# Two neighbouring steps of a Strassen-type double exchanged in the second feed-forward stage

## The chip, the core and the metric

The kernel runs on one core of a Trainium2 chip. The metric is the device time of one execution in microseconds (us). Its engines are named as in the profile: PE is TensorE, the matrix engine (PEld its weight loads), DVE is VectorE, ACT is ScalarE, POOL is GpSimd, and SP is SyncE, which here only issues DMA transfers. Each engine works through its own instructions in order, and they wait for one another through semaphores. Matmuls add into banks of PSUM, 128 partitions by 512 fp32 values each. ACT and DVE read the banks.

## What is computed

One encoder layer on 512 tokens of width 1024: a half-weighted gated feed-forward stage, a mixer (dilated window attention, grouped-query attention, gates), a second feed-forward stage, and a final normalisation. Only the second feed-forward stage matters here:

```python
def rmsnorm(x, g):
    xf = x.astype(jnp.float32)
    y = xf * lax.rsqrt(jnp.mean(xf * xf, axis=-1, keepdims=True) + EPS)
    return (y * g.astype(jnp.float32)).astype(x.dtype)

def swiglu(x, w1, w3, w2):
    return (jax.nn.silu(x @ w1) * (x @ w3)) @ w2
...
        x = x + hybrid_mixer(h, w_in[l], b_gate[l], q_norm[l], k_norm[l], rel_bias,
                             w_branch_a[l], w_branch_b[l], w_out[l], cos, sin)
        x = x + 0.5 * swiglu(rmsnorm(x, ffn2_norm[l]), ffn2_w1[l], ffn2_w3[l], ffn2_w2[l])
    return rmsnorm(x, final_norm)
```

x is 512 by 1024, w1 and w3 are 1024 by 2816, w2 is 2816 by 1024, all fp32.

## The kernel before

**Products.** Activations are kept with features on partitions and tokens along the free axis. Each fp32 operand is split into a high part and the rest (names end in H and L). A product is three matmuls: high by high (L258), high weights by low activations (L259), low weights by high activations (L260).

**Doubles.** The 2816 hidden features are 22 chunks of 128. The kernel takes two neighbouring chunks f and f + 1 of w1 and w3 as a 2 by 2 block product, the inner dimension and the tokens being halved too, and computes it in the Strassen-Winograd way, with seven block products in place of eight. This is called a double. Its seven steps are named A11, S1, S2, A12, S3, S4, A22; each is 24 matmuls of 128 by 256. A double uses three banks: A, which A11 opens and which S2, S3 and A22 add to; Y, which S1 opens and S4 adds to; X for A12. Bank A comes from a pool of four (in the profile: mm), X and Y from another pool of four (X, Y), out of which also come the bank of the statistic (stat) and that of its transposes (rb).

**Evictions.** After every step the bank's sum so far goes out (`evict`): ACT copies it after A11 (L510), S1 (L512) and S2 (L514), DVE adds it to such a copy after A12 (L516), S3 (L521) and S4 (L530), and multiplies after A22 (L538). After S4, L533 multiplies by R, the row norms, and L534 applies silu.

**Order.** PE runs in the order in which the program is written; `slots` makes it. Double number i of a group has its step j at slot 7i + 2j, so that two doubles interleave. In the first group of the second stage, `ahead` is true, and a list of numbers puts the first steps in another order. S1(2) below is step S1 of the double whose first chunk is 2.

**Weights.** The same list orders the weights, since each step needs its own 128 by 1024 tile. A11 and A12 are loaded as they are (raw tile wa); the tiles of S1 and S3 are the sum of two loads (wt: SP issues the first, and POOL one that adds onto it, L225); those of S2 and S4 are added on DVE (ws, L242: S2 from S1's and A11's raw tile, S4 from S2's and A12's); A22 is loaded (wr). Then ACT casts the raw tile to the high part (wh, L243) and DVE subtracts to get the rest (wl, L244). There is room for four prepared tiles. At each step the one of three steps later is prepared, and its cast waits until PE has done the step before. There is room for four raw wt tiles, three wa and two ws, and a load is issued when its room is free, in an order of due times (`turn_of`).

**Statistics.** After the fourth step of the first group PE sums squares (`stat_r`, stat, L424), DVE scales them (L416) and POOL raises them to the power -0.5 (r, L417). After the sixth step PE transposes r (`stat_R`, rb, L433) and ACT copies the result to R (L435). These two hooks go by the number of the step, whichever step it is. In the same stretch ACT and DVE still prepare the activations' halves and sums (hH, hL, TH, TL) for the stage.

Of the kernel before, what the change touches and what calls it, by code (L numbers as in the profile page):

```python
# [70 lines left out]
class Layer:  # L71
# [58 lines left out]
    @staticmethod  # L130
    def slots(fs, ahead=False):
        at = {7 * i + 2 * j: (f, step) for i, f in enumerate(fs) for j, step in enumerate(STEPS)}
        order = [at[k] for k in sorted(at)]
        if ahead:
            order[:5] = [order[n] for n in (0, 3, 4, 1, 2)]
        return order

    def ffn_order(self, s):
# [1235 lines left out]
```

## Time and profile before

| | |
|---|---|
| Median of three runs | 1250.46 us |
| Lowest and highest | 1250.18 and 1250.67 us |
| The profiled execution: its own time | 1250.19 us |
| Its span, first to last instruction | 1248.4 us |
| Mean granted clock of PE | 0.998 |
| First step of the first group of the second stage begins | 904.42 us |
| That group's doubles end, its w2 products begin | 984.47 us |

All times inside the execution are counted from the start of the span. The timeline gives an instruction's start and length. [...] A list of waits gives, for an engine's line, how long the engine stood idle before it and which instruction ended that; the latter is inferred from semaphores.

### The profile page before, as it was taken

The page shows a single profiled execution, that of the slowest core. Times are in us where ns is not written, and L with a number is a line of the kernel's source. Part 1 is how long each engine was busy: PE and PEld are TensorE (multiplying, and loading weights), DVE is VectorE, ACT ScalarE, POOL GpSimd, SP SyncE. Part 2 cuts the span into 40 slices and gives each one's busy share as a digit, 9 for nine tenths or more (in the row PEclk, how much of TensorE's full clock was granted, in tenths as well). Part 3 has the DMA queues.
Part 4 walks back from the last instruction along what each step waited for, and adds up shares of the span by engine and source line. Part 5 has one row for each costly group of instructions (what it writes and reads, how often), then busy time and mean ns, then how long its engine had stood idle before and what let it go on. Part 6 is the DMA issues. An engine that isn't in the chain of part 4 may idle for free.

```text
span 1248.4 us, 20502 instructions
## 1 busy us (share of the span) xinstructions
PE 1234.5 (99%) x8220; PEld 1115.5 (89%) x8220; DVE 908.1 (73%) x1373; ACT 603.5 (48%) x897; POOL 126.5 (10%) x132
## 2 busy tenths in 40 slices
PE   9999999999999999999999999999999999999997
PEld 7897999899899999978888878888899989988997
DVE  7784688468787887477755898865978747874874
ACT  8551355245464444454423446654565425532553
POOL 1111101000222110200000200000211001100001
PEclk9999999999999999999999999999999999999999
DMA  8875777241488982653343131167767536743222
GB/s 296 230 192 166 195 196 192 95 119 51 143 214 252 233 223 105 226 170 79 94 132 101 51 110 43 66 217 246 205 169 193 163 101 185 187 152 104 66 85 68
DMA packets 90656, 190.85 MB, mean 153 GB/s; under 512 B 12849, under 2 KB 19393, under 8 KB 90561
## 3 DMA queue, kind: packets, MB, share of 16 engines
q1 hardware_dynamic: 71344, 145.46, 34.8%
q0 software_dynamic: 18496, 43.54, 17.4%
q8 instruction: 64, 1.05, 0.4%
q10 hardware_dynamic: 720, 0.55, 0.1%
q14 instruction: 32, 0.25, 0.1%
HBM read 175.79 MB, written 17.38 MB: 155 GB/s over the span
## 4 chain that ended last, share of the span: by engine, by line
PE 94%; DVE 3%; issue 1%; ACT 1%; POOL 0%; DMA 0%; SPq 0%; POOLq 0%; DVEq 0%
PE mm L258 24%; PE mm L260 23%; PE mm L259 23%; PE Y L260 4%; PE Y L259 4%; PE Y L258 4%; PE X L259 2%; PE X L260 2%; PE X L258 2%; PE mm L979 1%; PE S L903 1%; PE Tb L1115 1%; PE T L990 1%; DVE wl L244 0%; PE Sb L260 0%
## 5 line engine op out<-in xcount | busy, mean ns | idle before, releaser
L243 ACT CAST wh<-wr 128x1024 fp32r<-128x1024 f32 x133 | 139.4, 1049 | 188.0 <-PE mm L259 124.0
L244 DVE TENSOR_TENSOR wl<-wr,wh 128x1024 fp32r<-128x1024 f32 x133 | 163.1, 1226 | 55.4 <-ACT wh L243 55.2
L258 PE MATMUL mm<-hH,wh 128*128 128x256 f32 (+1 forms) x560 | 179.8, 321 | 1.7 <-ACT c L514 1.5
L260 PE MATMUL mm<-hH,wl 128*128 128x256 f32 (+1 forms) x560 | 177.2, 316 | 0.9 <-DVE wl L244 0.9
L259 PE MATMUL mm<-hL,wh 128*128 128x256 f32 (+1 forms) x560 | 177.3, 317 | 0.2 <-DVE hL L400 0.2
L258 PE MATMUL mm<-gg,wh 128*128 128x512 f32 (+1 forms) x440 | 166.4, 378 | 0.0
L259 PE MATMUL mm<-gg,wh 128*128 128x512 f32 (+1 forms) x440 | 165.9, 377 | 0.0
L260 PE MATMUL mm<-gg,wl 128*128 128x512 f32 (+1 forms) x440 | 165.9, 377 | 0.0
L258 PEld LDWEIGHTS mm<-hH,wh 128*128 128x128 f32 x560 | 105.4, 188 | 11.0 <-ACT c L514 1.7
L260 PEld LDWEIGHTS mm<-hH,wl 128*128 128x128 f32 x560 | 105.3, 188 | 9.1 <-DVE wl L244 1.3
L259 PEld LDWEIGHTS mm<-hL,wh 128*128 128x128 f32 x560 | 105.5, 188 | 8.3 <-DVE hL L400 1.2
L243 ACT CAST wh<-wa 128x1024 fp32r<-128x1024 f32 x54 | 56.8, 1051 | 97.0 <-PE Y L259 47.1
L258 PEld LDWEIGHTS mm<-gg,wh 128*128 128x128 f32 x440 | 82.6, 188 | 16.6 <-PE mm L260 0.9
L260 PEld LDWEIGHTS mm<-gg,wl 128*128 128x128 f32 x440 | 82.6, 188 | 15.4
L259 PEld LDWEIGHTS mm<-gg,wh 128*128 128x128 f32 x440 | 82.6, 188 | 14.9
L243 ACT CAST wh<-ws 128x1024 fp32r<-128x1024 f32 x54 | 56.8, 1052 | 72.9 <-PE mm L259 51.4
L243 ACT CAST wh<-wt 128x1024 fp32r<-128x1024 f32 x54 | 56.8, 1052 | 67.7 <-PE mm L259 44.0
L258 PE MATMUL mm<-TH,wh 128*128 128x256 f32 x320 | 88.4, 276 | 0.0
L260 PE MATMUL mm<-TH,wl 128*128 128x256 f32 x320 | 88.3, 276 | 0.0
L259 PE MATMUL mm<-TL,wh 128*128 128x256 f32 x320 | 88.3, 276 | 0.0
L244 DVE TENSOR_TENSOR wl<-wt,wh 128x1024 fp32r<-128x1024 f32 x54 | 66.0, 1223 | 30.7 <-ACT wh L243 29.9
L244 DVE TENSOR_TENSOR wl<-wa,wh 128x1024 fp32r<-128x1024 f32 x54 | 66.0, 1221 | 25.2 <-ACT wh L243 25.1
(275 smaller groups left out, 3200.5 us busy)
## 6 DMA issues: line engine op xcount, KB each, us to landing
wr<-in_w2a SPq DMA_DIRECT2D x22, 512.0 KB, 3.3
wt<-in_w13b SPq DMA_DIRECT2D x22, 512.0 KB, 4.2
wa<-in_w13b SPq DMA_DIRECT2D x22, 512.0 KB, 3.6
wt<-in_w13b POOLq DMA_DIRECT2D x22, 512.0 KB, 5.9
wr<-in_w2b SPq DMA_DIRECT2D x22, 512.0 KB, 3.6
wt<-in_w13a SPq DMA_DIRECT2D x18, 512.0 KB, 3.4
wt<-in_w13a POOLq DMA_DIRECT2D x18, 512.0 KB, 6.3
wa<-in_w13a SPq DMA_DIRECT2D x18, 512.0 KB, 3.3
```

What stands on the lines that cost most here:

```text
L243: self.nc.scalar.copy(H, raw)
L244: self.nc.vector.tensor_sub(L, raw, f32(H))
L258: mm(out, lH, rH, start=start, stop=False, skip_group_check=more)
L259: mm(out, lH, rL, start=False, stop=False, skip_group_check=more)
L260: mm(out, lL, rH, start=False, stop=stop, skip_group_check=more)
L903: nc.tensor.matmul(*args, start=True, stop=True)
L979: nc.tensor.matmul(oc, v, p, start=st, stop=sp)
L990: nc.tensor.transpose(ps[:, 128 * b:128 * b + 128], P[h][:, c0 + 128 * b:c0 + 128 * b + 128], self.ident)
L1115: nc.tensor.transpose(pt[:, 128 * j:128 * j + 128], P[h, j][:, 128 * k:128 * k + 128], self.ident)
```

## The change

The table of numbers for the first group's order goes from five entries to seven. The first five are as before, the last two exchange the sixth and the seventh step:

```diff
         if ahead:
-            order[:5] = [order[n] for n in (0, 3, 4, 1, 2)]
+            order[:7] = [order[n] for n in (0, 3, 4, 1, 2, 6, 5)]
         return order
```

The group's first nine steps were A11(0), A12(0), A11(2), S1(0), S2(0), S3(0), S1(2), S4(0), S2(2). Now S1(2) is the sixth and S3(0) the seventh. Nothing else is moved by hand; the weights, their loads and the evictions follow the list.

PE, from the end of S2(0) to S4(0), before. A name's number tells tiles apart: mm_9203 is bank A of double 0, Y_9304 its Y, Y_9422 the Y of double 2. Each step's first and last rows stand here.

```order
L259 MATMUL mm_9203<-TL_8838,wh_9231 128x256
L260 MATMUL mm_9203<-TH_8837,wl_9232 128x256
L258 MATMUL mm_9203<-hH0_97,wh_9268 128x256 [waits Activation_49]
L260 MATMUL mm_9203<-hH3_100,wl_9269 128x256
L433 MATMUL rb_9412<-ident_84,r_90 128x128 [waits PE_49,Pool_49]
L258 MATMUL Y_9422<-TH_8837,wh_9300 128x256 [waits PE_49]
L260 MATMUL Y_9422<-TH_8837,wl_9301 128x256
L258 MATMUL Y_9304<-hH4_101,wh_9338 128x256
```

The same now; the Y of double 2 is Y_9387:

```order
L259 MATMUL mm_9203<-TL_8838,wh_9231 128x256
L260 MATMUL mm_9203<-TH_8837,wl_9232 128x256
L258 MATMUL Y_9387<-TH_8837,wh_9268 128x256 [waits PE_49]
L260 MATMUL Y_9387<-TH_8837,wl_9269 128x256
L433 MATMUL rb_9413<-ident_84,r_90 128x128 [waits PE_49,Pool_49]
L258 MATMUL mm_9203<-hH0_97,wh_9300 128x256 [waits Activation_49]
L260 MATMUL mm_9203<-hH3_100,wl_9301 128x256
L258 MATMUL Y_9304<-hH4_101,wh_9338 128x256
```

S2(0) and S3(0), both on mm_9203, no longer follow each other; the transposes stay between the sixth and the seventh step, and so stand ahead of S3(0) now.

ACT, around the eviction of S2(0) (L514), as the difference of the two orders:

```order
 L514 COPY c_9228<-mm 128x512 [waits PE_49]
 L243 CAST wh<-wr 128x1024 [waits DMAHW3_49,PE_49]
+L512 COPY c_9298<-Y 128x512 [waits PE_49]
 L435 COPY R<-rb 128x512 [waits PE_49]
 L243 CAST wh<-wa 128x1024 [waits DMAHW2_49,DVE_49,PE_49]
-L512 COPY c_9298<-Y 128x512 [waits PE_49]
 L243 CAST wh<-wa 128x1024 [waits DMAHW6_49,DVE_49,PE_49]
```

The eviction of S1(2) (L512 on c_9298) moves ahead of the copy of R and of one cast. On DVE, the eviction of S3(0) (L521) moves behind the next row of L244.

SP, the loads that change places, before: wt_9237 is S1(4)'s tile, wt_9346 S3(4)'s, wa_9385 A12(4)'s, wt_9382 S1(6)'s.

```order
L224 DMA wt_9237<-in_w13b 128x2x512 [waits DMAHW7_49,DMASW3_49,DVE_49]
L224 DMA wt_9346<-in_w13b 128x2x512 [waits DMAHW0_49,DMASW4_49,DVE_49]
L222 DMA wa_9385<-in_w13b 128x2x512 [waits DVE_49]
L224 DMA wt_9382<-in_w13b 128x2x512 [waits DMAHW2_49,DMASW5_49,DVE_49]
L222 DMA wr_9620<-in_w13b 128x2x512 [waits DMAHW3_49,DVE_49]
```

And now, S3(4)'s tile being wt_9377:

```order
L224 DMA wt_9237<-in_w13b 128x2x512 [waits DMAHW7_49,DMASW3_49,DVE_49]
L224 DMA wt_9377<-in_w13b 128x2x512 [waits DMASW4_49,DMAHW0_49,DVE_49,Activation_49]
L224 DMA wt_9382<-in_w13b 128x2x512 [waits DMASW5_49,DVE_49]
L222 DMA wa_9385<-in_w13b 128x2x512 [waits DMAHW2_49]
L222 DMA wr_9620<-in_w13b 128x2x512 [waits DMAHW3_49,DVE_49]
```

A12(4)'s load moves behind S1(6)'s. S3(4)'s tile takes the room of the first of the two exchanged wt tiles, which is S1(2)'s now and has one reader more, the sum for S2(2).

## The prediction

> **What bounds the kernel now.** I read the page's parts 1 and 4 first, to see which engine sets the time. Line one is busy time by engine, line two the shares of the chain that ended last.
>
> ```profile
> PE 1234.5 (99%) x8220; PEld 1115.5 (89%) x8220; DVE 908.1 (73%) x1373; ACT 603.5 (48%) x897; POOL 126.5 (10%) x132
> PE 94%; DVE 3%; issue 1%; ACT 1%; POOL 0%; DMA 0%; SPq 0%; POOLq 0%; DVEq 0%
> ```
>
> PE (TensorE) is busy for 99% of the span. A change that leaves the matmuls as they are can only win what PE idles, so the next view is PE's list of waits, cut to 900 to 960 us, where the second feed-forward stage begins (microseconds in total, times, longest).
>
> ```profile
> PE mm L258 <- ACT c L514: 1.5, 1, 1.5
> ```
>
> That is the whole list of that window: one wait, for a copy on ACT (ScalarE). The same list from 930 to 1230 us is empty. To see the steps I took the busy time by stretch, one step to a stretch: start and end, length, PE busy and its count, granted clock, DMA share, GB/s.
>
> ```profile
> 912.98:915.84 2.86, 2.86 (x27) 1.00 1.03 186
> 916.64:919.55 2.91, 2.91 (x26) 1.00 0.86 282
> 921.22:924.08 2.86, 2.86 (x24) 1.00 1.08 169
> 924.43:927.34 2.91, 2.91 (x27) 1.00 0.94 168
> 927.34:930.07 2.73, 2.73 (x27) 1.00 0.65 206
> 930.07:932.78 2.71, 2.71 (x26) 1.00 0.61 193
> ```
>
> In order these are S1(0), S2(0), S3(0), S1(2), S4(0), S2(2), the number in brackets being the double's first chunk. Between S1(0) and S2(0) stands the statistic's matmul (stat), between S3(0) and S1(2) the transposes (rb). Between S2(0) and S3(0) nothing stands, and yet 919.55 to 921.22 is empty. The timeline across that junction (start, length, engine, line, operation; in brackets the idle time before it and what ended it):
>
> ```profile
> 919.32 0.28 PE L259 MATMUL mm<-TL,wh 128*128 128x256 f32 x1
> 919.43 0.28 PE L260 MATMUL mm<-TH,wl 128*128 128x256 f32 x1
> 919.63 1.04 ACT L243 CAST wh<-ws 128x1024 fp32r<-128x1024 f32 x1 [2.19 <-PE mm L259]
> 920.58 0.58 ACT L514 COPY c<-mm 128x512 f32<-128x512 f32 x1
> 921.22 0.39 PE L258 MATMUL mm<-hH,wh 128*128 128x256 f32 x1 [1.50 <-ACT c L514]
> 921.44 0.29 PE L259 MATMUL mm<-hL,wh 128*128 128x256 f32 x1
> 921.56 0.28 PE L260 MATMUL mm<-hH,wl 128*128 128x256 f32 x1
> ```
>
> S2(0) and S3(0) add into the same bank. L514 must copy S2's sum out before S3 adds to it. ACT took the cast of a later step's weights first (919.63), because that stands ahead of the copy in its program; the copy ended at 920.58 + 0.58 = 921.16, and S3 began 0.06 later. So the wait is the copy's own 0.58 and the cast's 1.04.
>
> **The change part by part.** *The junction.* S1(2) now follows S2(0). It opens a bank of its own and does not need the copy. What it needs must be there at 919.55: its weights in both halves, now made fifth instead of sixth, and its bank. ACT's and DVE's rows for the fifth and sixth weights, and the reading of the bank X that later auxiliary tiles reuse:
>
> ```profile
> 910.23 1.05 ACT L243 CAST wh<-wt 128x1024 fp32r<-128x1024 f32 x1 [0.57 <-PE X L259]
> 911.34 0.68 DVE L516 TENSOR_TENSOR c<-X,c 128x512 f32<-128x512 f32 x1
> 911.94 1.22 DVE L244 TENSOR_TENSOR wl<-wt,wh 128x1024 fp32r<-128x1024 f32 x1
> 913.06 1.05 ACT L243 CAST wh<-wt 128x1024 fp32r<-128x1024 f32 x1 [1.05 <-PE mm L259]
> 915.07 1.22 DVE L244 TENSOR_TENSOR wl<-wt,wh 128x1024 fp32r<-128x1024 f32 x1
> ```
>
> The fifth weights are complete at 911.94 + 1.22 = 913.16, the sixth at 916.29: both before 919.55, whichever step owns them. X was read out by 912.02; its bank, next in the rotation of four, now goes to the transposes instead of S1(2), which takes one last used in the attention. Nothing holds S1(2). The gap from the last matmul of S2 to the next start falls from 921.22 - 919.43 = 1.79 to the usual 0.12 (919.32 to 919.43): **-1.67 us**.
>
> *The restart.* After the wait the first matmul took 0.22 to the next (921.22 to 921.44) instead of 0.12: **-0.10 us**. The same loss after the transposes passes from S1(2) to S3(0) and costs the same.
>
> *Pace.* The early steps ran slower than the later ones, 2.83 to 2.91 against 2.71 to 2.73, at a granted clock of 1.00 throughout. I do not know why, so I bound it. Without its restart S3(0) took 2.76 and S1(2) some 2.82, together 5.58. After the exchange each may run at 2.72 or at 2.83: 5.44 to 5.66, which is -0.14 to +0.08. I take **0**, the middle being near it.
>
> *S3(0), later.* It starts at about 919.55 + 2.82 + 0.35 for the transposes = 922.7. L514's copy, which needs only S2's end, is still done at 921.16, so its 1.04 of cast and 0.58 of copy now lie under S1(2), with 1.5 to spare. If that cover were gone, the first term would come back in full. Later still, A22(0) adds to the bank that S3(0)'s eviction (L521) reads; on DVE (VectorE) that row moves behind one weight row. Four steps and the transposes lie between the end of S2(0) and A22(0), and S3(0) is now the second of them, so two whole steps (5.4) remain for rows of 1.22 and 0.69. **0**.
>
> *The transposes.* They stand between the fifth and sixth steps either way, but start at 919.55 + 2.82 = 922.4 instead of 924.08. They need r from POOL (GpSimd):
>
> ```profile
> 916.99 1.23 DVE L244 TENSOR_TENSOR wl<-ws,wh 128x1024 fp32r<-128x1024 f32 x1
> 917.07 2.03 POOL L417 TENSOR_TENSOR r<-ms,mhalf 128x4 f32<-128x4 f32 x1 [5.11 <-DVE ms L416]
> 918.25 1.23 DVE L242 TENSOR_TENSOR ws<-ws,wa 128x1024 f32<-128x1024 f32 x1
> 920.71 1.23 DVE L244 TENSOR_TENSOR wl<-ws,wh 128x1024 fp32r<-128x1024 f32 x1 [1.23 <-ACT wh L243]
> 924.08 0.60 PE L433 MATMUL rb<-ident,r 128*128 128x128 f32 x4
> ```
>
> r is there at 917.07 + 2.03 = 919.10. The margin shrinks from 5.0 to 3.3 and stays positive: **0**. The copy of R on ACT moves behind S1(2)'s copy, one row of 0.58, and is used only by S4(0)'s eviction, a whole step later: 0.
>
> *The loads.* Three transfers change places on SP: S3(4)'s goes 2 us later, S1(6)'s stays, and A12(4)'s is issued after it instead of before. Issues by SP and POOL, the median landing of POOL's adding transfers from 900 to 960 us (last number), the first sum on DVE that uses S1(6)'s and A12(4)'s, and the next weights:
>
> ```profile
> 915.18 0.37 SPq L222 DMA_DIRECT2D wa<-in_w13b  x1
> 916.32 0.37 SPq L224 DMA_DIRECT2D wt<-in_w13b  x1
> 919.08 1.24 POOL L225 DMA_DIRECT2D wt<-in_w13b  x1
> 922.24 1.20 POOL L225 DMA_DIRECT2D wt<-in_w13b  x1 [1.93 <-DMA wt<-in_w13b]
> wt<-in_w13b POOLq DMA_DIRECT2D x6, 512.0 KB, 6.0
> 943.96 1.23 DVE L242 TENSOR_TENSOR ws<-wt,wa 128x1024 f32<-128x1024 f32 x1
> 945.70 1.21 DVE L244 TENSOR_TENSOR wl<-wr,wh 128x1024 fp32r<-128x1024 f32 x1
> 952.05 0.28 PE L260 MATMUL mm<-TH,wl 128*128 128x256 f32 x1
> ```
>
> The last adding transfer lands at about 922.24 + 6.0 = 928.2; its sum then runs at 943.96 - 1.77 = 942.2. That leaves 14 us, against shifts of about 2: **0**.
>
> The sum is -1.67 - 0.10 = **-1.77 us**, between -1.91 and -1.69 by the pace. PE's list being empty from 930 to 1230 us, all that follows starts earlier by the same amount; the tail after 1230 hangs on PE's last matmuls and moves with them. The profiled execution took 1250.19 us around a span of 1248.4, so it would take 1248.42. The median of the runs is 0.27 above it: 1250.46 - 1.77 = **1248.7 us**, or 0.14% less. I call 0.2% (2.5 us) the least that a measurement here tells from no change, so this counts as no change.
>
> **The rivals.** *B, the wait stays.* S1(2) waits for something else that ends about when the copy did, or loses the 1.67 elsewhere within the stretch. For it: L514 is named by inference. Against it: S3's start follows the copy's end by 0.06, and S1(2)'s known inputs are 6 us early. Time: 1250.5.
>
> *C, r comes late.* r took 2.03, and it ran beside DVE's rows at 916.99 and 918.25. If POOL and DVE shut each other out, r ran only after 918.22, in 0.88, and slipped ahead of the next row. Losing that race twice, it would end at 921.94 + 0.88 = 922.82, and the transposes would wait from 922.4: 0.4 of the gain lost, 1249.1. Against it: DVE stood idle for 1.23 before 920.71, so losing once gives 919.48 + 0.88 = 920.36, which costs nothing. [...]
>
> *D, slower: the sum at 943.96 waits for its load.* DVE runs in order, so the weights at 945.70 would wait behind it; they end at 946.91 and PE needs them at 952.05, a slack of 5.1. A stall of D us costs PE D - 5.1. It eats the gain at D = 6.9 and makes the kernel slower by 2.5 from D = 9.4, beyond 1253.0. The load would have to land 14 + 9.4 = 23 us late. Only an exchange of queue places speaks for it.
>
> *E, more than the wait.* If the three steps from 916.64 to 927.34 (10.70 with wait and transposes) all ran at 2.72, they would take 3 x 2.72 + 0.35 = 8.51: -2.19, 1248.3. To pass 2.5 the two steps ahead of them would have to gain as well, and those are not touched.
>
> **How the numbers follow.** The forecast has 0.86, B 0.05, C 0.02, D 0.03, E 0.04. The forecast's own range is 1248.2 to 1249.1: the pace's bounds and half of the 0.49 by which the three runs differ, on both sides. The whole range, 1247.9 to 1250.1, takes in C and E and reaches most of the way to B. Faster by over 0.2% means under 1247.96: half of E and a tail of 0.06 of the forecast, 0.08. Slower means over 1252.96: D and 0.01, 0.04. Within: 0.88.
>
> **What would show it.** Right: PE's waits from 900 to 960 us hold no row against L514; the copy still ends near 921.2 with S1(2)'s matmuls running over it; the transposes start near 922.4 and S4(0) near 925.6 instead of 927.34; the span is near 1246.6. Wrong: a wait of PE at S1(2)'s first matmul (B), one of rb for r (C), an idle DVE row for a wt load near 942 (D), or steps of 2.72 before S4(0) (E). The forecast fails if S4(0) starts earlier by 1.8 and the end does not.

## The result, and the profile after

In 22 runs of each kernel the median is 1248.63 us for the changed kernel (1248.12 to 1250.46) and 1250.7 us for the kernel before (1250.12 to 1251.76). The ratio is 0.9983, 95% interval 0.9977 to 0.9989. That is 2.1 us less, 0.17%. The interval leaves out 1, so the gain is clear of the noise, but it is no change by the prediction's bound of 0.2%, which the interval takes in. Of the runs further down, one at 2518.3 us (four copies, new order) and one at 1367.67 us (the weights' place) lie far outside all others and are left out of the medians. The profiled execution took 1248.49 us around a span of 1246.7, 1.70 less than before in both.

Parts 1 and 4 of the changed kernel's page:

```profile
PE 1234.0 (99%) x8220; PEld 1114.8 (89%) x8220; DVE 907.7 (73%) x1373; ACT 603.6 (48%) x897; POOL 126.6 (10%) x132
PE 94%; DVE 3%; ACT 1%; POOL 0%; issue 0%; DMA 0%; SPq 0%; POOLq 0%; DVEq 0%
```

PE is busy for the same share of the span, and "issue" fell from 1% to 0% in the chain. PE's list of waits between 900 and 960 us, which held L514 alone, is now empty, and L514 is gone from the list of the whole span too.

Busy time by stretch, columns as in the prediction. In order: S1(0), S2(0), S1(2), S3(0), S4(0), S2(2).

```profile
913.13:915.98 2.85, 2.85 (x26) 1.00 1.02 170
916.79:919.70 2.91, 2.91 (x26) 1.00 0.97 319
919.70:922.42 2.72, 2.72 (x26) 1.00 0.83 230
922.78:925.69 2.91, 2.91 (x28) 1.00 1.06 189
925.69:928.41 2.72, 2.72 (x27) 1.00 1.11 274
928.41:931.13 2.72, 2.72 (x27) 1.00 0.75 247
```

S2(0) and the step behind it now touch. The only gap left is that of the transposes, 922.42 to 922.78. From S2(0)'s start to S4(0)'s start took 10.70 us before (916.64 to 927.34) and takes 8.90 now (916.79 to 925.69): 1.80 less. S2(0) itself began 0.15 later in this execution and the rest of the span is 0.05 shorter, which makes the span's -1.70.

The timeline of the changed kernel across the junction (start, length, engine, line, operation):

```profile
919.58 0.28 PE L260 MATMUL mm<-TH,wl 128*128 128x256 f32 x1
919.70 0.28 PE L258 MATMUL Y<-TH,wh 128*128 128x256 f32 x1
919.78 1.05 ACT L243 CAST wh<-ws 128x1024 fp32r<-128x1024 f32 x1 [2.19 <-PE mm L259]
920.74 0.58 ACT L514 COPY c<-mm 128x512 f32<-128x512 f32 x1
922.42 0.60 PE L433 MATMUL rb<-ident,r 128*128 128x128 f32 x4
922.78 0.36 PE L258 MATMUL mm<-hH,wh 128*128 128x256 f32 x1
922.98 0.28 PE L259 MATMUL mm<-hL,wh 128*128 128x256 f32 x1
```

A matmul's row is longer (0.28) than the distance to the next one's start (0.12), so rows overlap, and what a matmul takes is counted from start to start. ACT does just what it did, the cast first and then the copy, at the same distance behind S2(0). The copy ends at 920.74 + 0.58 = 921.32, while PE works on S1(2). S3(0), which needs it, starts at 922.78, so the copy is ready 1.46 early.

### The profile page after: what moved, and what is told of

Read it like the earlier page. It is cut to its first block, busy times and chain, and to the rows that moved or that the text cites. A ratio compares the mean times of both kernels' runs of the same rounds, so it can differ in the third digit from the quotient of the medians.

```text
span 1246.7 us, 20502 instructions
## 1 busy us (share of the span) xinstructions
PE 1234.0 (99%) x8220; PEld 1114.8 (89%) x8220; DVE 907.7 (73%) x1373; ACT 603.6 (48%) x897; POOL 126.6 (10%) x132
## 3 DMA queue, kind: packets, MB, share of 16 engines
q8 instruction: 64, 1.05, 0.4%
## 4 chain that ended last, share of the span: by engine, by line
PE 94%; DVE 3%; ACT 1%; POOL 0%; issue 0%; DMA 0%; SPq 0%; POOLq 0%; DVEq 0%
PE mm L258 24%; PE mm L260 23%; PE mm L259 23%; PE Y L259 4%; PE Y L260 4%; PE Y L258 4%; PE X L259 2%; PE X L260 2%; PE X L258 2%; PE mm L979 1%; PE S L903 1%; PE Tb L1115 1%; PE T L990 1%; DVE wl L244 0%; PE Sb L260 0%; PE Sb L259 0%
## 5 line engine op out<-in xcount | busy, mean ns | idle before, releaser
L244 DVE TENSOR_TENSOR wl<-wr,wh 128x1024 fp32r<-128x1024 f32 x133 | 163.1, 1226 | 55.1 <-ACT wh L243 55.0
L244 DVE TENSOR_TENSOR wl<-wt,wh 128x1024 fp32r<-128x1024 f32 x54 | 66.0, 1223 | 30.7 <-ACT wh L243 30.0
L244 DVE TENSOR_TENSOR wl<-wa,wh 128x1024 fp32r<-128x1024 f32 x54 | 66.0, 1221 | 23.4 <-ACT wh L243 23.3
```

Of the source, the lines that this page charges most:

```text
L244: self.nc.vector.tensor_sub(L, raw, f32(H))
```

## The experiments

Theory 1 is the prediction's: PE idled because S3(0) adds to the bank that the copy of S2(0) reads, and that copy stood behind a cast on ACT; one step and the transposes now lie over both. Its rival, theory 2, was that the copy is only what the trace names, and that something else set S3(0)'s start or gave the gain, such as the place of the steps or the clock. Each difference below is against runs of the kernel before on the same chip, or against the changed kernel's 1248.63 where said, which may be of another chip.

### The copy first, in the old order

```diff
-        self.nc.scalar.copy(H, raw)
+        (self.cast_late if (name, key) == ("swb", (2, "S2")) else self.nc.scalar.copy)(H, raw)
...
-                nc.scalar.copy(hi, ps)
+                self.first = nc.scalar.copy(hi, ps)
...
+    def cast_late(self, H, raw):
+        with self.tc.issue_after(self.first.ins):
+            self.nc.scalar.copy(H, raw)
```

> The order of steps of before, with one thing changed: on ACT the copy that evicts S2(0) goes ahead of the cast of S2(2)'s weights. Theory (the bank is held by the copy, and the copy by the cast ahead of it): the copy starts at S2(0)'s end, about 919.8 us, and ends about 920.4; S3(0) starts near 920.4 instead of 921.22, PE's wait for the copy falls from 1.5 to about 0.7, and the time by 0.8 us, to 1249.9. Rival (the wait belongs to something else that ends at the same time, such as S3(0)'s weights or activations): S3(0) still starts at 921.2, the time stays at 1250.7.

The median was 1249.55 us against 1250.35, 0.80 less (ratio 0.9994, interval 0.9985 to 1.0003). ACT's timeline of this kernel, and the row of PE's waits:

```profile
919.65 0.58 ACT L514 COPY c<-mm 128x512 f32<-128x512 f32 x1 [2.31 <-PE mm L260]
920.13 1.05 ACT L1279 CAST wh<-ws 128x1024 fp32r<-128x1024 f32 x1
PE mm L258 <- ACT c L514: 0.7, 1, 0.7
```

With the two rows of ACT exchanged, the wait fell from 1.5 to 0.7, and S2(0) to S4(0) took 9.87 instead of 10.70. The cast had been a good half of the wait. The median's interval takes in no change; the size rests on the trace, and the median agrees.

### The bank of S2(0) not read out, in the old order

```diff
-                nc.scalar.copy(lo, ps)
+                [nc.scalar.copy(c, ps) for c in ((lo, hi) if s == "b" and not f else (lo,))]
...
-                nc.scalar.copy(hi, ps)
+                (s == "a" or f) and nc.scalar.copy(hi, ps)
```

> The order of steps of before; S2(0)'s bank is not evicted: the double's copy that should hold S2's sum is filled from the bank after A11 instead, so the w3 half of one double is computed from a wrong sum. Theory (the eviction alone holds S3(0) back): S3(0) follows S2(0) without a gap, at about 919.6; the time falls by the same 1.8 us as the exchange brings, to 1248.9. Rival (the gain of the exchange comes from something else that it moves, loads, the order on ACT, the place of the transposes): it stays at 1250.7, or moves by clearly less than 1.8.

The median was 1248.43 us against 1250.35, 1.92 less (ratio 0.9984, interval 0.9975 to 0.9993). This execution reached the group 1.05 later than the one before the change (905.47 against 904.42), so only distances compare. The stretches of S2(0), S3(0) and S1(2):

```profile
917.56:920.47 2.91, 2.91 (x27) 1.00 1.01 355
920.47:923.19 2.72, 2.72 (x27) 1.00 0.78 174
923.54:926.45 2.91, 2.91 (x27) 1.00 1.06 182
```

S3(0) touches S2(0), and the three steps with the transposes take 8.89, against the changed kernel's 8.90. In the old order, with the reading of S2(0)'s bank left out, the whole gain is there. Besides that the edit only adds a second copy behind A11(0), two steps and more ahead. Theory 2 has nothing left to explain.

### The copy made four times, in both orders

```diff
-                nc.scalar.copy(hi, ps)
+                [nc.scalar.copy(hi, ps) for _ in range(4 if s == "b" and not f else 1)]
```

In the old order:

> Before, with the copy that evicts S2(0) made four times in a row on ACT. Three more copies follow each other by about 0.48 us. Theory: S3(0) waits for the last of them, 1.44 us longer, from 921.22 to 922.7; the time grows by 1.4 us, to 1252.1. Rival (the copy does not decide): no change, 1250.7.

The median was 1253.37 us against 1250.35, 3.0 more (ratio 1.0024, interval 1.0015 to 1.0034). PE's wait, the copies, the first matmul behind them, and the stretches of the wait, of S3(0) and of S1(2):

```profile
PE mm L258 <- ACT c L514: 3.4, 1, 3.4
920.60 2.43 ACT L514 COPY c<-mm 128x512 f32<-128x512 f32 x4
923.08 0.58 PE L258 MATMUL mm<-hH,wh 128*128 128x256 f32 x1 [3.35 <-ACT c L514]
919.56:923.08 3.52, 0.17 (x3) 0.95 0.89 197
923.08:927.34 4.26, 4.26 (x25) 0.64 1.01 176
927.69:930.60 2.91, 2.91 (x27) 1.00 0.00 0
```

PE's wait follows the copies, as theory 1 says, and by their length: three more take 2.43 - 0.58 = 1.85, and the wait grew from 1.50 to 3.35. The expectation had them at 0.48 each, and they took 0.62. But S3(0) itself took 4.26 instead of 2.86, at a granted clock of 0.64. That 1.40 was in neither theory; 1.85 + 1.40 = 3.25, and S2(0) to S4(0) grew by as much, from 10.70 to 13.95.

In the new order:

> The changed kernel, with the copy that evicts S2(0) made four times in a row on ACT, 1.44 us more than once. Theory (S1(2) and the transposes cover the copy with 1.4 us to spare): the last copy ends about 922.8, when S3(0) is due; no wait or one of up to 0.15 us, time 1248.6 to 1248.8. Rival (the cover is thinner than that, since other evictions on ACT wait behind the copies): a wait of 0.5 us or more, 1249.1 or above.

The median was 1249.40 us, 0.95 under the kernel before (ratio 0.9992, interval 0.9982 to 1.0001, so a difference is not certain) and 0.8 above the changed kernel's. The copies, the transposes, the first matmul of S3(0), and the stretches of S3(0), S4(0) and S2(2):

```profile
920.42 2.44 ACT L514 COPY c<-mm 128x512 f32<-128x512 f32 x4
922.11 0.60 PE L433 MATMUL rb<-ident,r 128*128 128x128 f32 x4
922.91 0.39 PE L258 MATMUL mm<-hH,wh 128*128 128x256 f32 x1 [0.21 <-ACT c L514]
922.91:925.85 2.94, 2.94 (x25) 1.00 1.10 176
925.85:928.68 2.83, 2.83 (x27) 1.00 1.07 263
928.68:931.50 2.82, 2.82 (x26) 1.00 0.70 229
```

S3(0) was due 0.36 behind the transposes, at 922.47, and started at 922.91: 0.44 lost of 1.86 of extra copying. The cover had 1.46 to spare, and 1.86 - 1.46 = 0.40. So the cover is as wide as the prediction had it. The expectation had the three copies at 1.44, and with that the loss came out between its two theories; the median, 1249.40, lies where the rival had it, without the rival's mechanism. The next two steps ran at 2.83 and 2.82 instead of 2.72, which is another 0.2 without a cause that the trace names. From S2(0) to S4(0) the same copies cost 3.25 in the old order (10.70 to 13.95) and 0.48 in the new one (8.90 to 9.38); by the medians 3.0 and about 0.8.

### The copy made eight times, in the new order

The edit is the last one with 8 in place of 4.

> The changed kernel with the copy that evicts S2(0) made eight times; on ACT four of them follow each other, the others stand between S1(2)'s eviction, the copy of R and a cast, and the last ends near 926.8 us. Theory (S3(0) waits for the bank's last reader as soon as the cover is used up): S3(0) starts near 926.9 instead of 922.8, with a wait of about 4 us for that copy, time near 1252.8. Rival (the exchange has taken the copy off PE's path altogether): at most 0.5 us, 1249.1.

The median of three runs was 1255.78 us, 5.55 above the kernel before (ratio 1.0043, interval 1.0027 to 1.0059) and 7.1 above the changed kernel's 1248.63. PE's wait, the last copies, and the stretches of the transposes with the wait, and of S3(0):

```profile
PE mm L258 <- ACT c L514: 4.2, 1, 4.2
926.18 1.25 ACT L514 COPY c<-mm 128x512 f32<-128x512 f32 x2
922.67:927.48 4.81, 0.60 (x6) 0.84 1.05 185
927.48:932.76 5.28, 5.28 (x24) 0.50 0.42 115
```

The last copy ends at 927.43 and S3(0) starts at 927.48: with the cover used up, the copy decides again. S3(0) then ran wholly at half the clock, 5.28 instead of 2.91, and that 2.37 is most of what the expectation missed.

### Two and three copies, in the old order

These were to find from which length a wait costs more than itself. The edit is the same, with 2 and with 3. Two:

> Before, with the copy that evicts S2(0) made twice. With four copies PE waited 3.4 us and S3(0) then took 4.26 us, its first half at half the granted clock, in place of 2.86; with one copy the wait is 1.5 and S3(0) takes 2.86 at full clock. Between these the idle time must have a length from which the clock falls. A further copy adds about 0.62 us of wait. First theory (the clock falls only when PE was idle for about 3 us or more): wait 2.1, S3(0) 2.86, time 0.6 above before, 1250.9. Second theory (the slowing grows with the idle time from the start, a third of the surplus for each copy): wait 2.1, S3(0) near 3.3, 1251.4. [...]

The median was 1251.12 us against 1250.4, 0.72 more (ratio 1.0008, interval 0.9998 to 1.0017). The first matmul of S3(0) and that step's stretch:

```profile
921.80 0.38 PE L258 MATMUL mm<-hH,wh 128*128 128x256 f32 x1 [2.12 <-ACT c L514]
921.80:924.65 2.85, 2.85 (x24) 1.00 1.09 184
```

The wait grew from 1.50 to 2.12, the extra copy's 0.62, and S3(0) kept the full clock. That is the first theory, by the trace; its 3 us is the author's estimate, between the measured 1.50 and 3.35. The median's interval takes in no change. But three of the ten runs took 1251.90, 1252.40 and 1253.41, up to 2.3 above their median, and none of the three was profiled. Three:

> Before, with the copy that evicts S2(0) made three times. First theory (the clock falls from about 3 us of idle time): wait 2.7, S3(0) 2.86, time 1.2 above before, 1251.5. Second theory (the slowing grows with the idle time): wait 2.7, S3(0) near 3.8, 1252.5.

The median was 1253.48 us against 1250.4, 3.1 more (ratio 1.0022, interval 1.0013 to 1.0032). PE's timeline from the wait on, with the rows where the spacing changes, and S3(0)'s stretch:

```profile
923.04 0.39 PE L258 MATMUL mm<-hH,wh 128*128 128x256 f32 x1 [2.74 <-ACT c L514]
923.27 0.35 PE L259 MATMUL mm<-hL,wh 128*128 128x256 f32 x1
923.41 0.41 PE L260 MATMUL mm<-hH,wl 128*128 128x256 f32 x1
923.62 0.42 PE L258 MATMUL mm<-hH,wh 128*128 128x256 f32 x1
...
926.61 0.35 PE L260 MATMUL mm<-hH,wl 128*128 128x256 f32 x1
926.80 0.29 PE L258 MATMUL mm<-hH,wh 128*128 128x256 f32 x1
926.93 0.28 PE L259 MATMUL mm<-hL,wh 128*128 128x256 f32 x1
923.04:927.52 4.48, 4.48 (x25) 0.62 1.06 190
```

Here one matmul follows the other by 0.14, then from 923.41 by 0.21, and from 926.80 by 0.13. S3(0) took 4.48, 1.62 more than its 2.86. Neither expectation gave that. The ten runs fall into two groups. Two took 1251.50 and 1251.68, about 1.2 above the kernel before, which is the extra wait alone (2.74 - 1.50), at a mean granted clock of 0.998; the others took 1252.81 to 1254.90, at 0.995 to 0.997. So the same three copies seem at times to cost only the wait; neither of the two was profiled. In the two traces the slowing sets in between waits of 2.12 and 2.74, but with the longest runs of the two-copy kernel that is not shown to be a fixed length; the last section has more on this.

### The pace: the hooks one step later

The prediction had left open why the early steps ran at 2.83 to 2.91. Two more kernels looked at that, in the new order. The first moves the statistic and the transposes behind the next step.

```diff
-        self.ffn_run("b", G_FFN2, G_FIN, {3: self.stat_r, 5: self.stat_R}, out)
+        self.ffn_run("b", G_FFN2, G_FIN, {4: self.stat_r, 6: self.stat_R}, out)
```

> The changed kernel with the statistic and the transposes one step later each: stat after S2(0), the transposes after S3(0). It asks why the early steps are slow. First theory (a restart slows the step that follows it, until that step's end): S2(0) falls to 2.72 us and S3(0) to 2.72; S1(2), behind the statistic, and S4(0), behind the transposes, take 2.91 each; total unchanged within 0.2 us. Second theory (what counts is a step's place in the list: a slow pace ends only at the start of a step in an even place, the sixth or eighth): S2(0), the fifth, 2.83; S1(2), the sixth, 2.82 with its restart; S3(0), the seventh, 2.72; S4(0), the eighth, 2.82; total 0.2 to 0.3 us less. Both: r is ready about 1 us before the transposes at the latest, no new wait.

The median was 1248.13 us against 1250.23 (ratio 0.9985, interval 0.9975 to 0.9994), not to be told from the changed kernel. S2(0), S1(2) behind the statistic, S3(0), and S4(0) behind the transposes:

```profile
915.13:917.86 2.73, 2.73 (x27) 1.00 0.73 251
918.66:921.58 2.92, 2.92 (x27) 1.00 0.93 248
921.58:924.40 2.82, 2.82 (x26) 1.00 0.80 150
924.76:927.59 2.83, 2.83 (x28) 1.00 1.08 195
```

The loss at a restart went with the hook to S1(2), but S3(0) and S4(0) came out between the two values of the restart theory (2.72 and 2.91), and the theory of the place was right only at S4(0). Both fall.

### The pace: the weights' place in their tiles

Each prepared weight tile stands at one of two offsets, by the parity of its number in the order. Here the two are exchanged for the second stage alone; the order of the instructions is the same.

```diff
-            return 160 - 128 * (n % 2)
+            return 160 - 128 * ((n + (name[2] == "b")) % 2)
```

> The changed kernel with the offset of the prepared weights inside their tiles exchanged in the second stage between the steps in odd and in even places of the list. If the slow pace depends on that offset, the slow and fast steps change places: S2(0) 2.82 with its restart, S1(2) 2.83, S3(0) 2.82 with its restart, A11(2) 2.72. If it depends on restarts alone, all step lengths stay: S2(0) 2.91, S1(2) 2.72, S3(0) 2.91, A11(2) 2.83, and the total stays at 1248.6.

The median was 1248.67 us against 1250.23 (ratio 0.9987, interval 0.9976 to 0.9998). A11(2), S2(0), S1(2) and S3(0):

```profile
910.43:913.15 2.72, 2.72 (x26) 1.00 0.11 11
916.92:919.74 2.82, 2.82 (x27) 1.00 0.84 284
919.74:922.46 2.72, 2.72 (x27) 1.00 0.91 285
922.81:925.63 2.82, 2.82 (x27) 1.00 1.07 187
```

The offset theory gave three of these four; S1(2) should have slowed to 2.83 and stayed at 2.72. A11(2) says nothing, since it also ran at 2.72 in other traces with the old offsets, such as that of the hooks (909.46 to 912.18). S2(0) says more: behind the statistic it took 2.91 or 2.92 in every trace with the old offsets, and 2.82 here. So the place of the weights may have a part in the pace, on the word of one trace, but it is not the whole. What sets the pace stays open. At most 0.2 us per step hang on it.

## Why the prediction was right

*The junction, -1.67: right.* S2(0)'s last matmul starts at 919.58 and S1(2)'s first at 919.70, 0.12 later, where it had been 1.79. Reading the bank was the cause: without it the old order takes the same 8.89 (the experiment without the read-out). The cast's share was smaller than its length of 1.04: with the copy first, the wait fell by 0.82 (1.50 to 0.68), since the cast began before S2(0)'s sum was ready (919.63, the last matmul's row ending at 919.71) and its end overlaps the copy by 0.09. The sum used only the gap as a whole, so it is not touched. "Fifth" and "sixth" weights and steps in the prediction count from zero; they are the sixth and seventh of the list.

*The restart, -0.10: right.* After the transposes S3(0) pays 0.20 for its first matmul (922.78 to 922.98), and S1(2) pays nothing.

*The pace, 0 between -0.14 and +0.08: the bound held.* S1(2) and S3(0) took 2.72 + 2.91 = 5.63, or 5.55 without the restart, against the 5.58 of the middle. That one step ran at each pace, and the term so came out near 0, was luck: its cause was not known and is not now. Together the three terms gave -1.80 in this stretch, against the forecast's -1.77.

*S3(0) later, 0: right in size, incomplete in one sentence.* The copy was ready 1.46 early, forecast 1.5, and three extra copies found just that cover. But "If that cover were gone, the first term would come back in full" held here for waits of 1.50 and 2.12 alone. In the profiled executions a wait of 1.50 or 2.12 cost its own length; one of 2.74 cost 1.6 more, and 3.35 and 4.21 cost 1.4 and 2.4 more. The wait that the change removed, 1.50, was a cheap one, so the sum did not suffer. The prediction did not name this cost of a wait.

*The transposes and the loads, 0: right.* Rows of the changed kernel on which these two margins rest:

```profile
917.22 2.03 POOL L417 TENSOR_TENSOR r<-ms,mhalf 128x4 f32<-128x4 f32 x1 [5.11 <-DVE ms L416]
942.30 1.23 DVE L242 TENSOR_TENSOR ws<-wt,wa 128x1024 f32<-128x1024 f32 x1
```

r was there at 919.25 and needed at 922.42, a margin of 3.2 for the forecast 3.3, so C did not happen. No run shows that POOL and DVE shut each other out, as C supposes. Measured in the kernel before, L417 on 128 by 4 took 1.01 with no DVE row beside it (686.91), and 1.94 and 2.03 beside DVE rows of 1.22 and 1.23 (25.83 and 917.07), ending 0.89 and 0.88 after the row that it began beside. The sum on DVE ran at 942.30 (forecast 942.2) with no idle time ahead of it, so D did not. B is out with the empty list of waits. Of E, which had all three steps at 2.72, one ran so. The median's 2.1 lies nearer to E's 2.19 than the trace does, but its interval, 1.4 to 2.9 us, holds both, and the trace decides for 1.80. The stated range, 1248.2 to 1249.1, is 0.1 wider on each side than its own terms give (1248.3 to 1249.0); 1248.63 lies within both.

The sign that would have spoken against the forecast, S4(0) earlier by 1.8 and the end not, did not show: from S4(0)'s start to the end of the span took 321.06 before and 321.01 now.

## What to carry to other kernels

When a sum in a bank has to be read out between two steps that add to it, put a step on another bank between them, and measure the room from the last matmul to the end of the copy, with all that stands ahead of the copy on its engine. In these traces a row of PE's waits told what a stall cost up to 2.12 us and no longer from 2.74 on; read the granted clock of the step behind it as well. To prove that a wait comes from a certain row, lengthen that row in both orders: the order that hides it should lose only what goes beyond its cover.

## What the runs showed of the hardware

*In three traces slower matmuls followed a wait of PE.* After idle times of 1.50 us (the kernel before) and 2.12 (two copies) the granted clock over the next step was 1.00. After 2.74 (three copies) it was 0.62, after 3.35 (four, old order) 0.64, and after 4.21 (eight, new order) 0.50. Over the stretch of the wait it was 1.00, 0.95 and 0.84 in these three. The slow matmuls follow one another by 0.21 instead of 0.12: with three copies from 923.41, the two ahead of it having taken 0.23 and 0.14, to 926.61; with four from 923.46 to 926.02; with eight through the whole of S3(0). An estimate from these mean clocks, with the clock taken as either 1.00 or 0.50: it stood at half for 4.48 x 0.38 x 2 = 3.40 us with three copies, for 3.52 x 0.05 x 2 + 4.26 x 0.36 x 2 = 3.42 with four, and for 4.81 x 0.16 x 2 + 5.28 = 6.82 with eight, once and twice about the same length. By the same estimate PE had been idle for 3.35 - 0.35 = 3.00 when the clock fell with four copies, and for 4.21 - 1.54 = 2.67 with eight; with three copies it fell only after the 2.74 and the first matmuls. What makes it fall is not shown.

*So a wait's length alone did not tell what it cost.* The idle time ahead of the fall was not one length in the three traces, and the runs of one kernel differ: with three copies 1251.50 and 1251.68 at a mean granted clock of 0.998, against 1252.81 to 1254.90 at 0.995 to 0.997; with two copies 1251.90, 1252.40 and 1253.41 at 0.996 and 0.997, against 1250.37 to 1251.49 at 0.997 and 0.998. No trace shows a slow step behind 2.12 of idle time, nor a full clock behind 2.74.

*A copy repeated into the same tile took 0.62, one with another row behind it 0.48.* In the four-copy kernel of the old order each further one took 0.62 ((2.43 - 0.58) / 3). In the eight-copy kernel, where other rows of ACT stand between the later ones, a row starts 0.48 after such a copy (923.80 to 924.28). Why was not tried; the repeated copy reads the same bank and also writes the same tile.
